# Two neighbouring state blocks' output products issued together, term by term, in the S5 branch of a two-layer mixer block

## The chip, the cores and the metric

One core of a Trainium2 chip runs the whole program. The metric is device time in microseconds (us) of one execution; below, a time without a unit is in us. Engines: PE is TensorE (matrix products; PEld is its weight load), DVE is VectorE, ACT is ScalarE, POOL is GpSimd, SP issues the transfers.

## What is computed

The program is two layers on 256 tokens of width 1024. Each layer normalises, projects, runs four mixers side by side (dilated attention, NSA attention, gated linear attention or GLA, and S5), normalises the four results, projects them out, and ends with a feed-forward part (a SwiGLU in layer 0, eight experts in layer 1). The change is in S5, whose reference is, cut to what matters:

```
bu = einsum(ug, bb)                      # 16 groups x 64 complex states, per token
x_re, x_im = scan over tokens of x[t] = abar * x[t-1] + bu[t]
y = einsum('bsgn,gcn->bsgc', x_re, c_re) - einsum('bsgn,gcn->bsgc', x_im, c_im)
y = y + d * u;  hg = gelu(y);  return hg * sigmoid(hg @ glu_w + glu_b)
```

## The kernel before

All inputs of S5 are f32. The 16 x 64 states of a layer are 1024 rows, worked in eight **state blocks** m = 0 to 7 of 128 rows each. Per block (`m_s5`, lines 853 to 878): two products bring in the inputs (tile `s5b`, line 858, one PSUM buffer); DVE turns them into the rotating frame (lines 864 to 867, tiles `s5t` and a second `s5t` that is only scratch), runs two scans (line 870), and multiplies back: `p1` (named `s5p`, line 872, on DVE) and `z` (named `s5t`, line 873, on POOL, by the table `S5OUT`). Tiles `s5p` and `s5t` have two buffers each.

Then come the **output products** (lines 874 to 877): four f32 products, the *terms* 0 to 3, with a stationary operand of 128 rows x 32 columns. Term 0 and term 3 read `s5p`; terms 1 and 2 read `s5t`. All four accumulate into the same 32 partitions of the PSUM tile `s5y`; the quarter of the array's columns that they use is q = m mod 4 (`tile_position=(0, 32 * q)`). In the trace each f32 product is two matmul records (two passes).

Everything before the experts is placed by a list scheduler: the text of a layer is generated in the order of the string `ORDER`, one letter per step of a generator (S is a step of `m_s5`), and the scheduler then sets each engine's queue from its own estimates, with the projections (`w_...` tiles, 128x256 or 128x512 products) as work to fill in. Each engine then works its queue strictly in that order. Where a step's instructions change, the places of many others change with it. The feed-forward parts have an order written by hand.

`chid` (line 1154) is the other place that uses 32-column products: its neighbours go round all four column quarters.

Of the kernel before, what the change touches and what calls it, by code (L numbers as in the profile page):

```python
# [258 lines left out]
class Build:  # L259
# [565 lines left out]
    def m_s5(self):  # L825
        tc, nc, l, sp = self.tc, self.nc, self.l, self.sp
        v, g = nc.vector, nc.gpsimd
        mag = self.s5c[:, 0, 8 * l:8 * l + 8]
        fr = self.s5c[:, 1, 8 * l:8 * l + 8, None].to_broadcast([P, 8, 32])
        fi = self.s5c[:, 2, 8 * l:8 * l + 8, None].to_broadcast([P, 8, 32])  # L830
        cc = sp.tile([P, 3, 8, 32], F32, name="s5cc")
        t = sp.tile([P, 2, 8, 32], F32, name="s5ct", tag="s5p1", bufs=2)
        cr = self.par_("cr").rearrange("p (m c) -> p m c", m=8)
        ci = self.par_("ci").rearrange("p (m c) -> p m c", m=8)
        g.tensor_mul(t[:, 0], cr, fr)
        g.tensor_mul(t[:, 1], ci, fi)
        g.tensor_sub(cc[:, 0], t[:, 0], t[:, 1])
        g.tensor_sub(cc[:, 1], t[:, 1], t[:, 0])
        g.tensor_mul(t[:, 0], cr, fi)
        g.tensor_mul(t[:, 1], ci, fr)  # L840
        g.tensor_add(t[:, 0], t[:, 0], t[:, 1])
        g.tensor_scalar(cc[:, 2], t[:, 0], -1.0, None, op0=ALU.mult)
        if l:
            tab = self.tab
        else:
            with tc.issue_after(self.last_lo):
                tab = self.s5_tables(l, sp)
        yield
        uT = self.r["uT"]
        br = self.par_("br").rearrange("p (u n) -> p u n", u=2)  # L850
        bi = self.par_("bi").rearrange("p (u n) -> p u n", u=2)
        yp = self.ps("s", [P, 2, S], "s5y")
        for m in range(8):
            u, q = m // 4, m % 4
            rr = slice(32 * q, 32 * q + 32)
            b = self.ps("b", [P, 2, S], "s5b")
            for i, w in enumerate((br, bi)):
                nc.tensor.matmul(b[:, i], w[rr, u, :], uT[rr, u, :], start=True, stop=True, skip_group_check=True,  # L858
                                 tile_position=(32 * q, 0))
            cb = tab[:, 0, m, None, :].to_broadcast([P, 2, S])  # L860
            sb = tab[:, 1, m, None, :].to_broadcast([P, 2, S])
            z = sp.tile([P, 2, S], F32, name="s5t1", bufs=2)
            t2 = sp.tile([P, 2, S], F32, name="s5t2", bufs=1)
            v.tensor_mul(z, b, cb)
            v.tensor_mul(t2, b, sb)
            v.tensor_add(z[:, 0], z[:, 0], t2[:, 1])
            v.tensor_sub(z[:, 1], z[:, 1], t2[:, 0])
            mb = mag[:, m:m + 1].to_broadcast([P, S])
            for i in range(2):
                v.tensor_tensor_scan(z[:, i], mb, z[:, i], 0.0, op0=ALU.mult, op1=ALU.add)  # L870
            p1 = sp.tile([P, 2, S], F32, name="s5p1", bufs=2)
            S5OUT[0](nc).tensor_mul(p1, z, cb)
            S5OUT[1](nc).tensor_mul(z, z, sb)
            o = yp[32 * q:32 * q + 32, u, :]
            for i, (w, x) in enumerate(((0, p1[:, 0]), (1, z[:, 1]), (2, z[:, 0]), (2, p1[:, 1]))):
                nc.tensor.matmul(o, cc[:, w, m, :], x, start=i == 0, stop=i == 3, skip_group_check=True,  # L876
                                 tile_position=(0, 32 * q))
            yield
        y = sp.tile([P, 2, S], F32, name="s5yy", tag="s5t1", bufs=2)
        d = self.par_("s5d")  # L880
        for u in range(2):
            v.scalar_tensor_tensor(y[:, u], uT[:, u], d[:, u:u + 1], yp[:, u], op0=ALU.mult, op1=ALU.add)
        hg = sp.tile([P, 2, S], F32, name="s5hg")
        self.gelu(hg, y, [P, 2, S])
        yield
        gw = self.par_("gw").rearrange("p (k n) -> p k n", k=2)
        gb = self.par_("gb")
        gp = self.ps("a", [P, 2, S], "s5gp")
        zt = sp.tile([P, 2, S], F32, name="s5zt", tag="s5p1", bufs=2)
        for m in range(2):  # L890
            for k in range(2):
                self.mm(gp[:, m], gw[:, k, P * m:P * m + P], hg[:, k], k == 0, k == 1)
            v.tensor_scalar(zt[:, m], gp[:, m], gb[:, m:m + 1], None, op0=ALU.add)
        self.sigm(zt, zt, [P, 2, S])
        v.tensor_mul(hg, hg, zt)
        self.dump(f"y5{l}", hg)
        yield
        self.mixnorm(hg, 3)
        yield
# [956 lines left out]
```

## Time and profile before

| | us |
|---|---|
| median of 3 runs | 1447.29 (1445.8 to 1450.13) |
| the profiled execution | 1446.44 |
| its span, first to last instruction | 1444.6 |
| PE busy | 1400.3 (97%) |
| DVE busy | 891.3 (62%) |
| ACT busy | 703.8 (49%) |
| POOL busy | 120.4 (8%) |

Of the span, 86% of the chain that ended last is PE; PE's share at line 876, the products of this change, is 2%. S5's blocks run from about 67 to 126 us (layer 0) and from 400 to 457 us (layer 1). From 600 us on there are only experts. A busy PE is counted with overlaps and modelled ends, so the cost of a product is better read from the distance between starts, which the chain of waits gives.

### The profile page before, as it was taken

To read this page: it belongs to the slowest core of one execution; us is meant where nothing else is said; L and a number is where in the kernel's file an instruction comes from. 1 tells how busy PE (TensorE), PEld (TensorE's weight loads), DVE (VectorE), ACT (ScalarE), POOL (GpSimd) and SP (SyncE) were. 2 spreads that over 40 slices of the span, in tenths; PEclk is the share of its full clock that TensorE was granted. 3 is DMA by queue.
4 is the path that set the end of the run, shared out by engine and by line. 5 is a ranking of instruction groups with operands and counts; after the bars stand their busy time and mean duration, and the time that the engine had idled before them with its cause. 6 is when DMAs were issued, how large, how long until landed. Compare 5 with 4: busy or idle time off the path is not lost.

```text
span 1444.6 us, 19381 instructions
## 1 busy us (share of the span) xinstructions
PE 1400.3 (97%) x7189; PEld 966.2 (67%) x7189; DVE 891.3 (62%) x1371; ACT 703.8 (49%) x1090; POOL 120.4 (8%) x100
## 2 busy tenths in 40 slices
PE   8899899999999998999999999999999999999997
PEld 6667789999867877765566555566555566655652
DVE  8876878555696676864556554556554556455541
ACT  5436466444524744754454544554544554445430
POOL 3235300000222223000000000000000000000000
PEclk9999999999999998999999999999999999999999
DMA  8513085554325217789999999999999999999992
GB/s 336 189 53 134 30 304 194 188 177 146 110 98 229 89 69 323 286 346 416 419 421 421 379 388 403 421 422 420 388 388 400 420 422 421 411 413 407 421 421 108
DMA packets 61731, 434.58 MB, mean 301 GB/s; under 512 B 7360, under 2 KB 7616, under 8 KB 9664
## 3 DMA queue, kind: packets, MB, share of 16 engines
q1 hardware_dynamic: 61200, 432.73, 74.5%
q8 instruction: 58, 0.95, 0.3%
q10 hardware_dynamic: 432, 0.56, 0.1%
q14 instruction: 41, 0.34, 0.1%
HBM read 432.22 MB, written 1.05 MB: 300 GB/s over the span
## 4 chain that ended last, share of the span: by engine, by line
PE 86%; DVE 7%; issue 2%; ACT 2%; POOL 1%; DMA 0%; ACTq 0%; DVEq 0%; POOLq 0%
PE mgu L271 20%; PE my L271 18%; PE mgus L271 14%; PE fgu L271 8%; PE fy L271 4%; DVE wlo L309 2%; PE s5y L876 2%; PE acc L271 2%; PE mht L1628 2%; PE w_gv L271 2%; PE mgat L271 1%; PE mco L271 1%; PE s5b L858 1%; PE w_dq L271 1%; PE w_dk L271 1%
## 5 line engine op out<-in xcount | busy, mean ns | idle before, releaser
L309 DVE TENSOR_TENSOR wlo<-raw,whi 128x1024 fp32r<-128x1024 f32 x447 | 542.1, 1235 | 212.3 <-ACT whi L306 208.4
L306 ACT ACTIVATE whi<-raw 128x1024 fp32r<-128x1024 f32 x456 | 471.4, 1057 | 217.1 <-PE my L271 43.2
L271 PE MATMUL mgu<-whi,X 128*128 128x512 f32 x892 | 290.2, 399 | 0.0
L271 PE MATMUL mgus<-raw,Xf 128*64 128x512 f32 x896 | 213.3, 597 | 0.0
L271 PEld LDWEIGHTS mgu<-whi,X 128*128 128x128 f32 x892 | 169.0, 189 | 40.7 <-issue 2.2
L271 PE MATMUL mgu<-wlo,X 128*128 128x512 f32 x446 | 179.7, 403 | 0.8 <-DVE wlo L309 0.8
L271 PEld LDWEIGHTS mgus<-raw,Xf 128*64 128x64 f32 x896 | 63.4, 137 | 118.5 <-issue 113.5
L271 PE MATMUL my<-raw,mhx 128*64 128x512 f32 x448 | 105.6, 599 | 0.6 <-DVE mhx L1644 0.6
L271 PEld LDWEIGHTS mgu<-wlo,X 128*128 128x128 f32 x446 | 84.6, 190 | 20.3 <-DVE wlo L309 1.4
L271 PE MATMUL fgu<-flo,whi 128*128 128x256 f32 x344 | 96.5, 281 | 0.2 <-DVE flo L537 0.2
L271 PE MATMUL fgu<-fhi,wlo 128*128 128x256 f32 x344 | 96.4, 280 | 0.0
L271 PE MATMUL fgu<-fhi,whi 128*128 128x256 f32 x344 | 96.3, 280 | 0.0
L1635 ACT ACTIVATE mhh<-mht 128x512 fp32r<-128x512 f32 x28 | 16.7, 597 | 159.2 <-PE mht L1628 159.2
L271 PE MATMUL my<-wlo,mhh 128*128 128x512 f32 x224 | 89.1, 398 | 0.3
L271 PE MATMUL my<-whi,mhl 128*128 128x512 f32 x224 | 88.9, 397 | 0.0
L271 PE MATMUL my<-whi,mhh 128*128 128x512 f32 x224 | 74.7, 407 | 0.0
L1636 DVE TENSOR_TENSOR mhl<-mht,mhh 128x512 fp32r<-128x512 f32 x28 | 19.3, 690 | 88.3 <-ACT mhh L1635 88.3
L1621 DVE TENSOR_TENSOR mh<-mh,mgu 128x512 f32<-128x512 f32 x28 | 19.3, 688 | 82.8 <-PE mgu L271 82.8
L271 PEld LDWEIGHTS my<-raw,mhx 128*64 128x64 f32 x448 | 30.3, 136 | 58.3 <-issue 50.5
L271 PEld LDWEIGHTS fgu<-flo,whi 128*128 128x128 f32 x344 | 64.7, 188 | 0.8 <-DVE flo L537 0.4
L271 PEld LDWEIGHTS fgu<-fhi,whi 128*128 128x128 f32 x344 | 64.6, 188 | 0.4
L271 PEld LDWEIGHTS fgu<-fhi,wlo 128*128 128x128 f32 x344 | 64.6, 188 | 0.0
(479 smaller groups left out, 2069.5 us busy)
## 6 DMA issues: line engine op xcount, KB each, us to landing
raw<-in_moe SPq DMA_DIRECT2D x335, 1024.0 KB, 10.6
raw<-in_ffn SPq DMA_DIRECT2D x32, 1024.0 KB, 4.8
raw<-in_win SPq DMA_DIRECT2D x19, 1024.0 KB, 4.9
raw<-in_cw SPq DMA_DIRECT2D x8, 1024.0 KB, 4.9
raw<-in_wout SPq DMA_DIRECT2D x8, 1024.0 KB, 6.8
ca<-in_ca SPq DMA_DIRECT2D x2, 1152.0 KB, 8.6
par<-in_par SPq DMA_DIRECT2D x2, 1081.5 KB, 12.1
gbig<-in_cg SPq DMA_DIRECT2D x2, 864.0 KB, 6.7
```

Of the source, the lines that this page charges most:

```text
L271: self.nc.tensor.matmul(out, lhsT, rhs, start=start, stop=stop, skip_group_check=True)
L306: self.last_hi = self.nc.scalar.activation(hi, r, AF.Copy).ins
L309: self.last_lo = eng.tensor_sub(lo, r, hi.bitcast(F32)).ins
L858: nc.tensor.matmul(b[:, i], w[rr, u, :], uT[rr, u, :], start=True, stop=True, skip_group_check=True, tile_position=(32 * q, 0))
L876: nc.tensor.matmul(o, cc[:, w, m, :], x, start=i == 0, stop=i == 3, skip_group_check=True, tile_position=(0, 32 * q))
L1621: later(lambda p=p: v.tensor_mul(h, h, p))
L1628: nc.tensor.transpose(t[:, j], h[:, j * P:j * P + P], idn)
L1635: later(lambda: nc.scalar.activation(hh, t, AF.Copy))
L1636: later(lambda: v.tensor_sub(hl, t, hh.bitcast(F32)))
```

## The change

The four output products of a block are no longer issued at the end of the block. Blocks are taken in pairs (0 and 1, 2 and 3, ...). The even block only keeps its operands; at the end of the odd block the eight products of both are issued term by term, even block first: term 0 of m, term 0 of m+1, term 1 of m, and so on. Neighbours in this order use different column quarters. Products, operands, sizes and buffers are the same.

```diff
+        pair = []
         for m in range(8):
...
-            o = yp[32 * q:32 * q + 32, u, :]
-            for i, (w, x) in enumerate(((0, p1[:, 0]), (1, z[:, 1]), (2, z[:, 0]), (2, p1[:, 1]))):
-                nc.tensor.matmul(o, cc[:, w, m, :], x, start=i == 0, stop=i == 3, skip_group_check=True,
-                                 tile_position=(0, 32 * q))
+            pair.append((m, ((0, p1[:, 0]), (1, z[:, 1]), (2, z[:, 0]), (2, p1[:, 1]))))
+            for i in range(4) if m % 2 else ():
+                for n, terms in pair:
+                    w, x = terms[i]
+                    q = n % 4
+                    nc.tensor.matmul(yp[32 * q:32 * q + 32, n // 4, :], cc[:, w, n, :], x, start=i == 0, stop=i == 3,
+                                     skip_group_check=True, tile_position=(0, 32 * q))
+            if m % 2:
+                pair = []
             yield
```

What the scheduler makes of it, at three places. First PE's queue at the first pair of layer 0; `s5p_939` and `s5t_931` are block 1 before:

```order
L876 MATMUL s5y<-s5p_939,s5cc 32x256
L271 MATMUL w_dk<-hhi,wlo 128x256
L271 MATMUL w_dk<-hhi,whi 128x256
L271 MATMUL w_dk<-hlo,whi 128x256
L271 MATMUL w_dk<-hhi,wlo 128x256
L876 MATMUL s5y<-s5t_931,s5cc 32x256 x2
L876 MATMUL s5y<-s5p_939,s5cc 32x256
```

In the changed program, on PE at the same pair, `s5p_921` and `s5t_913` are block 0, `s5p_935` and `s5t_927` block 1:

```order
L880 MATMUL s5y<-s5p_935,s5cc 32x256
L880 MATMUL s5y<-s5t_913,s5cc 32x256
L1125 MATMUL nt_967<-id,p_966 128x128
L880 MATMUL s5y<-s5t_927,s5cc 32x256
L880 MATMUL s5y<-s5t_913,s5cc 32x256
L880 MATMUL s5y<-s5t_927,s5cc 32x256
L880 MATMUL s5y<-s5p_921,s5cc 32x256
L880 MATMUL s5y<-s5p_935,s5cc 32x256
```

Block 0's term 0 still goes early and alone (some rows above); the other seven products of the pair now alternate. Each of the eight pairs reads like this: one product alone, then seven that alternate, in one piece (4 pairs) or cut by other work into two and five (4 pairs).

Second, PE's queue at the end of layer 0's S5. Before, block 7 (its inputs are this `s5b`) is only wanted some 40 rows further down, after the two w_gv projections, and block 6 (`s5p_1183`, `s5t_1175`) is next:

```order
L858 MATMUL s5b<-uT,par 128x256 x2
L271 MATMUL qms<-qsq,cst 128x512
L876 MATMUL s5y<-s5p_1183,s5cc 32x256
L1138 MATMUL nt_1193<-id,p_1192 128x128 x2
L271 MATMUL ns_1309<-kz,nqn 128x512
L876 MATMUL s5y<-s5t_1175,s5cc 32x256 x2
L876 MATMUL s5y<-s5p_1183,s5cc 32x256
```

In the changed program the same stretch of PE's queue, with block 7 as `s5p_1288` and `s5t_1280`:

```order
L859 MATMUL s5b<-uT,par 128x256 x2
L880 MATMUL s5y<-s5p_1183,s5cc 32x256
L271 MATMUL qms<-qsq,cst 128x512
L271 MATMUL ns_1309<-kz,nqn 128x512
L271 MATMUL ckc<-chT,par 128x16 x2
L271 MATMUL gz<-par,ag 128x128 x2
L880 MATMUL s5y<-s5p_1288,s5cc 32x256
L880 MATMUL s5y<-s5t_1175,s5cc 32x256
L880 MATMUL s5y<-s5t_1280,s5cc 32x256
```

Block 7's products have moved ahead of the w_gv projections, to a few rows behind the products that bring in its inputs.

Third, PE's queue where layer 0's GLA begins, behind the last projection (w_gr). `gd` and `gL` are GLA's first products, `s5gp` is S5's gate, `ds` and `dt` are dilated attention. Before:

```order
L271 MATMUL gd<-cst,gqk 128x4 x2
L271 MATMUL gL<-gbig,glz 128x2x128 x2
L271 MATMUL s5gp<-s5hg,par 128x256 x2
L271 MATMUL ds_1453<-kz,qn 128x256 x2
L271 MATMUL gL<-gbig,glz 128x2x128 x2
```

After, on PE at the same place:

```order
L271 MATMUL s5gp<-s5hg,par 128x256 x2
L271 MATMUL ds_1453<-kz,qn 128x256 x2
L271 MATMUL s5gp<-s5hg,par 128x256 x2
L271 MATMUL gd<-cst,gqk 128x4 x2
L271 MATMUL ds_1476<-kz,qn 128x512
L1048 MATMUL dt_1465<-id,p_1456 128x128
L271 MATMUL ds_1494<-kz,qn 128x512
L1048 MATMUL dt_1465<-id,p_1456 128x128
L271 MATMUL gL<-gbig,glz 128x2x128
```

GLA's first `gL` has moved behind S5's gate and behind all three score products of dilated attention.

## Rows read from the trace of the kernel before

**Rows 1.** The page's slices: busy tenths of PE in 40 equal slices of the span

```profile
PE   8899899999999998999999999999999999999997
```

**Rows 2.** Stretches: us, then busy us (count) per engine, granted clock, DMA share, GB/s

```profile
67.00:126.00 59.00, 59.00 (x301) 36.77 (x293) 42.27 (x98) 23.82 (x62) 23.44 (x17) 1.00 0.29 105
126.00:189.00 63.00, 55.82 (x307) 45.33 (x308) 48.61 (x97) 35.33 (x83) 25.11 (x17) 1.00 0.24 86
189.00:380.00 191.00, 188.97 (x1323) 174.44 (x1321) 116.98 (x184) 98.96 (x156) 2.32 (x3) 1.00 0.53 189
...
400.00:457.00 57.00, 56.89 (x369) 38.75 (x368) 46.44 (x74) 15.13 (x27) 14.81 (x13) 1.00 0.38 141
457.00:503.00 46.00, 46.00 (x285) 38.65 (x284) 29.79 (x72) 35.53 (x79) 9.60 (x8) 1.00 0.38 144
...
600.00:1444.60 844.60, 831.44 (x3669) 497.22 (x3667) 460.95 (x476) 398.05 (x499) 0.00 (x0) 1.00 0.96 395
```

The busy columns are PE, PEld, DVE, ACT and POOL.

**Rows 3.** The chain of waits in order of time: start, us, engine, tile, records

```profile
76.29 0.55 PE s5y L876 x2
...
77.51 1.41 PE s5y L876 x6
...
96.29 1.84 PE s5y L876 x8
...
406.17 0.67 PE w_nq L271 x4
...
408.25 2.09 PE w_nq L271 x16
```

**Rows 4.** Tile s5y's records: count, ns min/median/max, first and last start

```profile
L876 PE MATMUL s5y<-s5p,s5cc x64: 379/379/404, 67.8 to 452.1; 128*32 128x256 f32 x64
```

There is a second row like it, for the terms that read s5t, with 64 records too.

**Rows 5.** The chain again, where products go round all four column quarters

```profile
66.09 1.86 PE chid L271 x32
```

**Rows 6.** Tile s5t's records, as in Rows 4: POOL's part of a block

```profile
L873 POOL TENSOR_TENSOR s5t<-s5t,s5tab x16: 1269/1281/3338, 64.5 to 449.2; 128x512 f32<-128x512 f32 x16
```

**Rows 7.** Timeline of DVE, layer 0's kz and layer 1's block 7: start, us, instruction

```profile
111.19 0.75 DVE L1028 SCALAR_TENSOR_TENSOR kz<-w_dk,par,qr 128x512 f32<-128x512 f32 x1 [1.82 <-ACT qr L331]
...
445.08 0.69 DVE L864 TENSOR_TENSOR s5t<-s5b,s5tab 128x512 f32<-128x512 f32 x1 [1.56 <-PE s5b L858]
...
448.38 0.69 DVE L872 TENSOR_TENSOR s5p<-s5t,s5tab 128x512 f32<-128x512 f32 x1
```

**Rows 8.** The chain in layer 0, products that now stand ahead of block 7

```profile
107.97 1.06 PE qms L271 x2
...
109.95 0.86 PE ns L271 x2
...
115.88 0.44 PE gz L271 x4
```

**Rows 9.** Timeline of ACT and DVE: steps of S5's gelu, layers 0 and 1

```profile
132.30 0.73 ACT L812 ACTIVATE s5hg<-s5hg,one 128x512 f32<-128x512 f32 x1
...
452.57 0.87 DVE L882 SCALAR_TENSOR_TENSOR s5yy<-uT,par,s5y 128x256 f32<-128x256 f32 x2 [0.97 <-PE s5y L876]
...
457.50 0.43 DVE L810 TENSOR_SCALAR s5hg<-s5hg 128x512 f32<-128x512 f32 x1
```

**Rows 10.** The chain in layer 1 at S5's gate

```profile
463.47 0.86 PE s5gp L271 x4
```

**Rows 11.** Timeline of layer 0 where GLA begins, several engines

```profile
133.11 0.53 PEld L271 LDWEIGHTS gd<-cst,gqk 128*128 128x128 f32 x4
...
135.15 0.60 ACT L942 ACTIVATE gE<-gL 128x512 f32<-128x512 f32 x1
...
136.80 4.40 POOL L952 TENSOR_TENSOR gQ<-gq,gE 128x512 f32<-128x512 f32 x2
```

**Rows 12.** Weight loads at the round of quarters: the tile's records, and the timeline

```profile
L271 PEld LDWEIGHTS chid<-raw,blk x128: 106/110/155, 43.3 to 447.5; 128*32 128x32 f32 x128
...
66.02 1.45 PEld L271 LDWEIGHTS chid<-raw,blk 128*32 128x32 f32 x32
```

## The prediction

> **What bounds the kernel now.** I read the slices first: PE is at eight or nine tenths nearly everywhere [rows 1]. Then the stretches, with their granted clock: it is 1.00, the full 2.4 GHz, in all of those shown. In S5's two, PE is busy all the time (59.00 of 59.00 us, 56.89 of 57.00), and so it is in what follows them, the feed-forward of layer 0 (188.97 of 191) and the rest of layer 1's projections (46.00 of 46) [rows 2]. So time that S5 gives back on PE can reach the end, as long as PE does not start to wait. DVE comes second: 42.27 of 59 us in layer 0 and 46.44 of 57 in layer 1 [rows 2]. The stretch from 126 to 189 us is different: PE has 7 us idle there, and GLA's recursion goes through ACT, POOL and DVE. The experts from 600 us on are PE's too (831.44 of 844.60), and their first loads follow the end of the mixers, so they should move as a whole.
>
> **What a product costs.** The output products are two rows of 64 records, 128 in all [rows 4]: 64 products, two records each. In the chain one product takes 0.55, three take 1.41, four take 1.84 [rows 3]: 0.43 for each further product, so a run of them costs 0.43 a product and 0.12 to begin. Coming back to full-width work costs too: 4 products of w_nq behind a run take 0.67 and 16 take 2.09 [rows 3], that is 0.118 a product and 0.20 once. A run thus costs 0.32 besides its products. All of it lies on PE's path.
>
> **What alternating gives.** The trace before has no two neighbours in two quarters, but it has four: in chid, 32 records, which are 16 products of the same shape, take 1.86 [rows 5]. Less 0.12 that is 0.109 a product, a quarter of 0.43. So four quarters run at once, and I take it that two quarters run two at once: 0.43 for two products. The bounds are 0.43 a product (nothing overlaps) and 0.215; chid is the nearest row, so I take 0.215 where two neighbours can pair.
>
> **The sum on PE.** Before, 64 x 0.43 = 27.5, in 29 runs counted in PE's order (14 and 15), x 0.32 = 9.3: 36.8. After, each of the eight pairs is one product alone (0.43) and seven that alternate, which make four steps of 0.43 (the seventh has no partner; cut into two and five it is one and three steps): 2.15 a pair, 17.2 in all; the runs are 20 (10 and 10), 6.4. That is 23.6, and 13.2 less. In two places the two input products of a block are cut apart by other work, which adds two runs, 0.6. **Gross: 12.6**, of it about 6.1 in layer 0 and 6.5 in layer 1.
>
> **What is given back.** The pair brings new waits. Term 1 of the odd block reads a tile that POOL writes in 1.28, starting when DVE ends `s5p` [rows 6]. PE starts the seven at that moment, has one step (0.55) to do and then waits, with all its queue behind it: 1.28 + 0.07 (a hand-over) - 0.55 = 0.8 where nothing stands between, less where a cut puts other work there. By the order that is 0.5 (an nt product between), 0.1 and 0.8 for layer 0's first three pairs, and 0.8, 0.2, 0.8, 0.2 in layer 1, where before the first block already stood about 0.4 for POOL: 1.4 and 1.6 net. Before, this wait was covered by three or four projection products, and in several pairs the cover is gone.
>
> The last pair of layer 0 is worse. Block 7's inputs come in only just ahead of its products. From them DVE takes 4.0 to the end of `s5p` (445.08 to 448.38 + 0.69 for the same block of layer 1, undisturbed) [rows 7]; a `kz` operation of 0.75 [rows 7] stands in its queue between, and I add 0.05 for the hand-over: 4.8. PE has in between one product alone with its run (0.75), qms 0.86 to 1.06, ns 0.86, ckc about 0.35 and gz 0.44 [rows 8]: 3.3. So PE waits 1.5, then 0.8 more for POOL: 2.3. Bounds: 1.0, if `kz` costs nothing, and 4.0 if POOL is as slow as its slowest record, 3.34.
>
> S5's gate in layer 1: from the last `s5y`, whose end released `s5yy` at 452.57 [rows 9], to `s5gp` at 463.47 [rows 10] PE had 11 us of other work. By its new order it has 45 products of w_dk at 0.118, qms and gz: 5.3 + 0.9 + 0.4, some 6.7. The gelu between takes 5.4 to the end of line 810 (457.93) [rows 9], then three ACT steps of up to 0.73 [rows 9] and a multiplication like those of a block, 2.7 at most: 8. That leaves 1.3; since weight splits queued among these steps may move, I put 1.0, between 0 and 2.
>
> The two buffers of `s5t`: the next pair's first operation on DVE (line 865 now) overwrites a tile that the pair's term 2 must have read, so DVE stands in its queue until PE is there, and behind it stand weight splits that PE's projections need. By the order one or two such splits and other work stand ahead of it in layer 1, which covers the 2.3 that POOL and two steps of PE take. I put nothing; without that cover it is 1 to 2 a pair (a rival below). Transfers: SP's order is the same, nothing moves there.
>
> Given back: 1.4 + 2.3 + 1.6 + 1.0 = 6.3, between 3 and 9. **Net 6.3**: 2.4 in layer 0, 3.9 in layer 1.
>
> **The GLA stretch of layer 0.** There the order changed beyond S5. Before, GLA's first `gE` came 2.0 after the last projection product (133.11 to 135.15), and POOL's `gQ` was then busy to 141.2 [rows 11]. Now the first `gL` stands behind S5's gate (4 records, 0.86, twice), ds three times (0.86 each), gd and dt, and `gE` behind the attention's exponentials on ACT: about 9 after the last projection product instead of 2. Against it, the attention, S5's gate and the gelu are then out of the way of the later steps. It is a recursion in which every step waits for ACT, POOL, PE and DVE in turn, with 7 us of PE idle. I take nothing for it, with -2 to +7 as bounds.
>
> **Sum.** Against its own time, the profiled execution's 1446.44 becomes 1446.44 - 6.3 = 1440.1. It lies 0.85 below the median of the runs, so the median should be **1441.0**, 0.44% faster. A change of 0.3% (4.3) is about what a measurement of this kernel can tell from none.
>
> **Rivals.** *GLA's late start eats layer 0's gain.* For: `gE` is 7 later relative to the projections and the recursion has few parallel branches. Against: the branches that it competed with are done earlier. If 4 to 7 of the 7 reach the end of the stretch, layer 0 loses 1.6 to 4.6 and layer 1 still gains 3.9: 1445 to 1448, within 0.3%. 20%.
>
> *DVE becomes the bound through the two buffers: slower.* In layer 1 DVE's 46.44 make 11.6 a pair, against 14.25 a pair of the stretch [rows 2]. If the standing adds over 2.65 a pair, DVE sets the pace. POOL's 1.28 and PE's two steps add 2.3; with POOL slowed by DVE to 3.34 [rows 6] it is 4.4, so 1.7 a pair, 7 in layer 1, instead of a gain; with layer 0's 2.4 left the time is about 1452. What speaks against it is the work queued ahead of the blocked operation, and that the slow record of POOL is one of 16. 10%.
>
> *No overlap of two quarters.* The products would stay at 0.43 each; only the nine runs fewer remain (2.3 net of the cut input products), which the waits take back: 1447. The Trainium skill, TensorE: Matmul & The Clock Gate, Part 3, has a rule that speaks for it: a weight load overlaps with matmuls in flight only when the row group differs. All eight products of a pair use the same rows. By that rule the loads would stand open and take the overlap back. What the rows show, as a mechanism here: the 32 loads of chid, also all of the same rows, last 0.11 each, 3.5 in all, but are done within 1.45 [rows 12], less than the 1.86 of the products [rows 5]. So by the trace the loads do not stand open, and I leave it 4%.
>
> *More than forecast.* If the waits are covered, or the GLA stretch gains by what was cleared ahead of it, up to 12.6 and 2 more: 1433 to 1435. 8%.
>
> **How the numbers follow.** The forecast, a gain of 4.3 to 12, has 58%; with the last rival faster by over 0.3% is 66%. Within 0.3%: 20 + 4 = 24%. Slower: 10%. The range goes from 1435 (a gain of 12, most waits covered) to 1448 (GLA's late start in full).
>
> **What would show it.** In the changed trace, seven alternating products take about 1.84 in the chain where four took 1.84; their records start in twos, 0.215 apart. Line 880 takes about 24 of PE's path with its switches, not 37. PE shows waits for POOL at line 874 of up to 0.8 in most pairs, and one of about 1.5 for `s5p` near the end of layer 0's S5. Layer 0's feed-forward starts 2 to 3 earlier and the router of layer 1 6 earlier; the experts take as long as now. I am wrong if records in two quarters start one after the other, if DVE idles at line 865 for over 1 a pair, or if the GLA stretch of layer 0 grows by more than 3.

## The result

The change made the kernel slower: 1455.41 us (1453.34 to 1457.65) against 1447.18 (1445.8 to 1450.13), a ratio of 1.0056 [1.0045, 1.0066]. I had forecast 1441.0, within 1435 to 1448. The profiled execution has a span of 1455.6 us against 1444.6. One traced execution can lie some us from its kernel's median (e3's, below, took 1447.21, its median is 1443.01), so below the medians say how much, and the traces where.

The page's slices of the changed kernel (40 slices of 36.4 us; PE's busy tenths, and the granted clock in tenths of full speed) answer [rows 1]. They differ in the fourth to the sixth slice, from 109 to 218 us, where PE is at 8, 7 and 8 instead of 9, 8 and 9; in the fourth the clock is at 8:

```profile
PE   8898789999999998999999999999999999999997
...
PEclk9998999999999998999999999999999999999999
```

The stretches say more. The columns are those of [rows 2]: busy time of PE, PEld, DVE, ACT and POOL, granted clock, DMA share, GB/s:

```profile
67.00:126.00 59.00, 54.95 (x310) 34.38 (x309) 46.31 (x102) 22.24 (x59) 20.23 (x15) 0.97 0.23 87
126.00:189.00 63.00, 51.97 (x266) 43.17 (x265) 41.84 (x85) 30.87 (x73) 26.92 (x17) 0.89 0.17 60
133.00:142.50 9.50, 9.47 (x58) 9.45 (x59) 2.21 (x4) 4.42 (x9) 1.69 (x1) 0.70 0.20 83
142.50:160.00 17.50, 15.77 (x70) 12.26 (x68) 8.70 (x27) 11.28 (x29) 9.24 (x7) 0.80 0.17 60
400.00:457.00 57.00, 55.41 (x401) 42.18 (x400) 46.73 (x73) 18.89 (x31) 12.28 (x13) 0.99 0.34 119
457.00:503.00 46.00, 45.80 (x289) 36.72 (x288) 31.51 (x76) 31.49 (x72) 9.21 (x8) 1.00 0.44 173
```

PE now has 4.05 us idle in S5's stretch of layer 0, where it had none, and from 126 to 189 the clock is 0.89 on average instead of 1.00 [rows 2]. Between 133 and 160 us PE is nearly always busy (9.47 of 9.50, 15.77 of 17.50) at 0.70 and 0.80: by these means some 13 of the 27 us were at 1.2 GHz, half speed.

The chain of waits (start, us, what) shows the place where it turns:

```profile
119.91 1.27 PE s5y L880 x4
121.19 1.81 PE w_gv L271 x6
...
125.71 2.89 DVE s5hg L821
...
128.62 2.46 DVE s5hg L810
...
131.11 0.64 ACT s5hg L811
...
131.77 0.72 ACT s5hg L812
132.49 0.49 ACT gv L750
...
133.03 1.86 PE w_gr L271 x7
```

S5's products are done at 121.2, some four us earlier than before, and gv's at 128.6. PE has a few small products left, up to 129.6, and then stands still for the evacuation of gv by ACT (line 750), since w_gr is to be written into a buffer that gv holds (timeline of PE):

```profile
133.03 0.58 PE L271 MATMUL w_gr<-whi,hhi 128*128 128x256 f32 x1 [3.40 <-ACT gv L750]
```

ACT could have evacuated at 128.6, but in its queue two steps of S5's gelu (lines 811 and 812) now stand ahead, and they wait for DVE. The timeline of ACT in the kernel before, and then in the changed one (start, us, instruction, and in brackets what ended ACT's idle time):

```profile
122.66 1.29 ACT L750 ACTIVATE gv<-w_gv 128x512 f32<-128x512 f32 x2 [0.58 <-PE w_gv L271]
...
131.66 0.61 ACT L811 ACTIVATE s5hg<-s5hg 128x512 f32<-128x512 f32 x1
```

```profile
131.11 0.63 ACT L811 ACTIVATE s5hg<-s5hg 128x512 f32<-128x512 f32 x1 [3.77 <-DVE s5hg L810]
131.77 0.72 ACT L812 ACTIVATE s5hg<-s5hg,one 128x512 f32<-128x512 f32 x1
132.40 1.06 ACT L750 ACTIVATE gv<-w_gv 128x512 f32<-128x512 f32 x2
```

Before, gv was evacuated right behind its products, and the gelu came 9 us later. Now the gelu is first, ACT idles 3.77 for it, and PE waits for ACT. It could pass gv because S5 now ends before gv's products do, and that the change itself has done.

The gelu was late for a reason of its own, too. Its two steps on DVE (lines 821 and 810) stood beside two weight splits of POOL. The timelines of POOL and of DVE in the changed kernel, and then DVE's before:

```profile
125.62 2.41 POOL L309 TENSOR_TENSOR wlo<-raw,whi 128x1024 fp32r<-128x1024 f32 x1 [7.26 <-ACT whi L306]
128.00 2.79 POOL L309 TENSOR_TENSOR wlo<-raw,whi 128x1024 fp32r<-128x1024 f32 x1
```

```profile
125.71 2.88 DVE L821 TENSOR_TENSOR s5hg<-s5hg,s5yy 128x512 f32<-128x512 f32 x1
128.62 2.45 DVE L810 TENSOR_SCALAR s5hg<-s5hg 128x512 f32<-128x512 f32 x1
```

```profile
127.74 0.69 DVE L821 TENSOR_TENSOR s5hg<-s5hg,s5yy 128x512 f32<-128x512 f32 x1
...
130.72 0.41 DVE L810 TENSOR_SCALAR s5hg<-s5hg 128x512 f32<-128x512 f32 x1
```

With 0.69 and 0.41 in place of 2.88 and 2.45 the gelu's two steps on ACT would have been through at about 128.6, just as gv's products end, and PE, busy to 129.6, would not have waited. That is an estimate from these rows; no run takes the splits out of the changed kernel.

All the kernels below are compared by four stretches, each from one profiled execution, read from the first and last records of w_qag, w_gr, x (line 639) and w_uT: **S** from the last w_qag to the first w_gr of layer 0 (S5's stretch, with the wait), **W** the products of w_gr, **G** from there to the first addition to x (GLA, attention, output), and **L1**, in layer 1, from the first w_uT to the last w_gr (S5's stretch there). The last column is the granted clock in S and in G.

| kernel | S | W | G | S+W+G | L1 | clock in S, G |
|---|---|---|---|---|---|---|
| before | 59.9 | 7.4 | 55.1 | 122.4 | 86.8 | 1.00, 1.00 |
| changed | 64.7 | 9.4 | 60.9 | 135.0 | 82.6 | 0.96, 0.94 |
| e1, pairs in layer 1 | 59.8 | 7.4 | 55.1 | 122.4 | 83.4 | 1.00, 1.00 |
| e2, pairs in layer 0 | 63.2 | 9.4 | 62.6 | 135.2 | 86.9 | 0.99, 0.92 |
| e3, gelu behind gv | 61.0 | 6.8 | 57.5 | 125.3 | 83.3 | 0.97, 0.97 |
| e4, not alternated | 66.7 | 9.4 | 62.5 | 138.6 | 86.8 | 0.99, 0.92 |
| e5, GLA late | 59.6 | 6.8 | 62.3 | 128.7 | 83.3 | 1.00, 0.95 |
| e6, before, gv behind gelu | 68.8 | 7.4 | 48.2 | 124.4 | 87.0 | 1.00, 1.00 |
| e7, GLA early | 61.2 | 6.8 | 60.9 | 128.9 | 82.6 | 0.97, 0.92 |
| e8, filled wait | 67.4 | 5.9 | 60.2 | 133.5 | 82.6 | 1.00, 0.97 |
| e9, GLA's first step early | 60.1 | 6.8 | 62.1 | 128.9 | 83.3 | 1.00, 0.89 |
| e10, GLA among w_gr | 60.1 | 12.5 | 57.6 | 130.2 | 82.5 | 1.00, 0.91 |
| e11, e3 with other terms | 59.5 | 6.8 | 56.5 | 122.8 | 82.3 | 1.00, 1.00 |
| e12, e10 with other terms | 61.0 | 12.5 | 57.6 | 131.1 | 81.8 | 0.97, 0.91 |
| e13, e11 with splits on DVE | 59.5 | 6.8 | 56.4 | 122.7 | 82.3 | 1.00, 1.00 |
| e14, e1 with other terms | 59.9 | 7.4 | 55.1 | 122.4 | 82.6 | 1.00, 1.00 |

So the changed kernel gains 4.2 in layer 1 and loses 12.6 in layer 0: 3.4 in the wait, 1.4 in the rest of S, 1.9 in W and 5.8 in G. The 1.4 is the clock's, in this trace: from 117 to 121 us it was 0.65. In e2, with the same order of PE and ACT in layer 0 and the same waits, it was 1.00 there, and S without the wait is 59.8. The stretch in the changed kernel, then in e2:

```profile
117.00:121.00 4.00, 3.19 (x14) 1.03 (x14) 1.36 (x6) 1.09 (x4) 1.27 (x1) 0.65 0.36 126
```

```profile
117.00:121.00 4.00, 3.99 (x21) 2.72 (x22) 1.67 (x5) 1.53 (x5) 0.00 (x0) 1.00 0.65 221
```

G is 56.5 or less in every trace with its clock at 1.00 there, and 57.5 or more in every other. So a part of what G loses below may be the clock's and not the order's; no run tells the two apart.

### The profile page after: what moved, and what is told of

It is laid out like the page before. It is cut to its first block, busy times and chain, and to the rows that moved or that the text cites. A ratio compares the mean times of both kernels' runs of the same rounds, so it can differ in the third digit from the quotient of the medians.

```text
span 1455.6 us, 19381 instructions
## 1 busy us (share of the span) xinstructions
PE 1398.8 (96%) x7189; PEld 968.5 (67%) x7189; DVE 895.5 (62%) x1371; ACT 703.8 (48%) x1090; POOL 118.7 (8%) x100
## 4 chain that ended last, share of the span: by engine, by line
PE 84%; DVE 9%; ACT 3%; issue 2%; DMA 1%; POOL 1%; SPq 0%; ACTq 0%; POOLq 0%; DVEq 0%
PE mgu L271 20%; PE my L271 18%; PE mgus L271 14%; PE fgu L271 8%; PE fy L271 4%; DVE wlo L309 2%; PE acc L271 2%; PE mht L1634 2%; PE mgat L271 1%; PE mco L271 1%; PE s5y L880 1%; PE w_gv L271 1%; ACT whi L306 1%; PE w_gr L271 1%; PE w_dq L271 1%
## 5 line engine op out<-in xcount | busy, mean ns | idle before, releaser
L1627 DVE TENSOR_TENSOR mh<-mh,mgu 128x512 f32<-128x512 f32 x28 | 19.2, 687 | 82.5 <-PE mgu L271 82.5
L271 PEld LDWEIGHTS fgu<-flo,whi 128*128 128x128 f32 x344 | 64.7, 188 | 0.8 <-DVE flo L537 0.4
```

The source lines that it names most:

```text
L271: self.nc.tensor.matmul(out, lhsT, rhs, start=start, stop=stop, skip_group_check=True)
L1627: later(lambda p=p: v.tensor_mul(h, h, p))
```

## The experiments

The theories: **A**, the order on ACT behind S5 in layer 0 makes the loss, by PE's wait at w_gr and the lower clock behind it; **B**, the pairs' own waits eat the gain, in either layer; **C**, GLA's late start in layer 0 is the loss.

**e1, pairs in layer 1 alone, and e2, in layer 0 alone.**

```diff
-            for i in range(4) if m % 2 else ():
+            for i in range(4) if m % 2 or not l else ():
...
-            if m % 2:
+            if m % 2 or not l:
                 pair = []
```

(e2 has `or l` in both lines.)

> Pairs in layer 1 alone; layer 0 issues as in the kernel before. Theory A (the loss is made in layer 0, behind S5: the gelu's ACT steps stand ahead of gv's two evacuations, PE waits 3.4 for them and then runs at a lower clock): layer 1 keeps its 3.7, so 1447.2 - 3.7 = 1443.5, 0.997 of before. Theory B (the pairs' own waits for POOL and DVE eat the gain wherever a pair stands, and layer 1's 3.7 only came from its starting 14.8 later): 1447, no difference. Theory C (GLA's late start in layer 0 is the loss): as A, 1443.5.

> Pairs in layer 0 alone; layer 1 issues as before. Theories A and C: all of the loss and none of layer 1's gain: 1455.4 + 3.7 = 1459, 1.008 of before; the first gE comes about 10 after the last w_gr. Theory B: half of a loss that both layers share, 1451.

Measured: e1 1443.8 us, 0.9974 [0.9963, 0.9984]; e2 1461.15, 1.0100 [1.0081, 1.0120]. In e1 stretches S, W and G are those of the kernel before; in e2 PE waits 3.4 at w_gr again, and L1 is that of before. So layer 1's gain is real and does not come from a late start there, the whole loss is layer 0's, and theory B falls as its cause. In layer 0 it holds for the gain, though: S without the wait is 59.8 in e2, where before has 59.9.

**e3, the gelu's ACT steps behind gv's evacuations (layer 0).**

```diff
+            self.gvi = nc.scalar.activation(gv[:, T], pv[T], AF.Copy).ins
-            nc.scalar.activation(gv[:, T], pv[T], AF.Copy)
...
-        self.gelu(hg, y, [P, 2, S])
+        with ExitStack() as cx:
+            if not l:
+                cx.enter_context(tc.issue_after(self.gvi))
+            self.gelu(hg, y, [P, 2, S])
```

> The changed kernel with one bound more: in layer 0 the gelu's ACT steps are issued behind gv's two evacuations. Theory A: PE's 3.4 ahead of w_gr is gone and with it the fall of the clock behind it, so the last w_gr is back within 2 of the kernel before's 133.1 (it was at 142.4): 9 to 11 come back, 1444 to 1446. Theory B: the pairs are untouched, so the time stays at 1455. Theory C: only what GLA's order gains; PE's wait ahead of w_gr goes but the clock does not come back, 1449 to 1452, and the stretch from the last w_gr to the mixers' end still takes 61.

Measured: 1443.01 us, 0.9968 [0.9959, 0.9977]: 12.4 less than the changed kernel. ACT's timeline and the stretches behind it:

```profile
127.00 1.31 ACT L750 ACTIVATE gv<-w_gv 128x512 f32<-128x512 f32 x2 [0.98 <-PE w_gv L271]
```

```profile
126.00:133.00 7.00, 7.00 (x56) 6.63 (x55) 5.53 (x11) 4.90 (x11) 4.11 (x3) 1.00 0.53 188
133.00:142.50 9.50, 7.99 (x44) 6.17 (x43) 6.89 (x17) 7.41 (x15) 7.66 (x5) 1.00 0.49 181
```

gv is evacuated as soon as its products are there, PE is busy all the time from 126 to 133, and the clock is 1.00 there and up to 142.5. The last w_gr ends at 135.3 instead of 142.4. But the edit also moved GLA: its first gE starts 5.5 behind the last w_gr, against 9.9 in the changed kernel and about 2 in the one before, and other steps of the attention and GLA with it. So e3 alone does not tell theory A from C; e5 does.

**e4, the pairs without alternating.**

```diff
-            for i in range(4) if m % 2 else ():
-                for n, terms in pair:
+            for n, terms in pair if m % 2 else ():
+                for i in range(4):
```

> The products of a pair stay behind the odd block's scan in the program, but block by block, so that neighbours share a column quarter; PE's queue has block 7 ahead of gv's second half as in the changed kernel, and the gelu's ACT steps ahead of gv's evacuations. If alternating is worth what I put (0.43 for two): eight pairs by 3 steps of 0.43 more, 10.3, less the waits of the pairs that go, 3 to 6, so 1459 to 1463 by theory A, which keeps the loss behind S5. Theory B (the waits of alternating pairs are the loss): those are gone and the time is back at 1447 or less. Theory C: as A.

Measured: 1464.81 us, 1.0112 [1.0090, 1.0134], a little above what I expected. It has the changed kernel's order on ACT, the 3.4 at w_gr and a clock of 0.64 and 0.81 behind it, and nothing of the gain: L1 is 86.8, as before. Against it the changed kernel is 9.4 faster, which is what alternating is worth: the table shows 7.8 of it, 3.6 in layer 0 and 4.2 in layer 1. So the overlap works, and what costs is the grouping of the blocks.

**e5, e3 with GLA late, as in the changed kernel.** The first gE is issued behind the attention's second `pt` on ACT.

```diff
+            with ExitStack() as cx:
+                if not self.l and lp == 0:
+                    cx.enter_context(tc.issue_after(self.dpt))
+                nc.scalar.activation(E, L.rearrange("p a b c -> p a (b c)"), AF.Exp, scale=1.0 / 16)
-            nc.scalar.activation(E, L.rearrange("p a b c -> p a (b c)"), AF.Exp, scale=1.0 / 16)
...
+            pti = nc.scalar.activation(pt, t, AF.Copy).ins
+            self.dpt = pti if tl == 0 else self.dpt
-            nc.scalar.activation(pt, t, AF.Copy)
```

> The kernel of e3, in which PE's wait ahead of w_gr is gone, but with GLA's first exponential held back behind the attention's second evacuation on ACT, where the changed kernel has it (gE 9.9 after the last w_gr instead of e3's 5.5). If GLA's late start has a price of its own (theory C as a second part of the loss), the stretch from the last w_gr to the mixers' end grows from e3's 57.5 to about 62 and the time from 1443 to 1447 or 1448. If the wait and the clock were all of it (theory A alone), the stretch stays within 1 of e3's and the time at 1443.

Measured: 1448.01 us, 1.0002 [0.9992, 1.0012], 5.0 above e3. G grew from 57.5 to 62.3, with no wait at w_gr and the clock at 1.00 from 126 to 142.5. The first gE came 11.9 behind the last w_gr, two us later than in the changed kernel, and steps of the attention changed places on ACT with it. So theory C is a second part of the loss: of the 12.4 between e3 and the changed kernel some 5, at that delay, belong to the order with GLA late, and the other 7 to the wait and the clock.

**e6, the kernel before with gv behind the gelu, without any pair.** gv's evacuation is written behind the gelu, which moves p_gr there too.

```diff
+        if not self.l:
+            yield
...
+            if not self.l:
+                cx.enter_context(self.tc.issue_after(self.gelu_ln))
...
-"...NvvSDNCrSMSDDDGG..."
+"...NvvSDNCSvrMSDDDGG..."
```

> The kernel before, without any pair, with gv's evacuations of layer 0 issued behind the gelu's first two ACT steps; GLA's first gL move ahead of w_gr on PE by it, so GLA starts no later than before. Theory A, in its strong form (the order on ACT alone makes the loss, whatever S5's products cost): PE waits 5 or more ahead of w_gr, the clock falls behind it, the last w_gr ends about 9 later than 133.4; GLA's early start gives up to 4 back: 1451 to 1456. If the pairs are needed for the loss: 1447, no wait at w_gr and a clock of 1.00 from 133 to 160.

Measured: 1449.8 us, 1.0014 [1.0005, 1.0024]. The first half came as expected: of PE's waits, and of its chain,

```profile
PE w_gr L271 <- ACT gv L755: 4.0, 1, 4.0
```

```profile
134.04 7.42 PE w_gr L271 x48
```

The order on ACT makes this wait without any pair, and the last w_gr ends 8.1 later. But the time rose by 2.2 only: with gv late, gL and gE had gone ahead of w_gr, and G shrank by 7 to 48.2, more than the 4 that I had allowed. So the order on ACT is enough for the wait; most of the loss did not come with it where GLA was early.

**e7, e3 with GLA ahead of S5's gate and the attention.**

```diff
-"...NvvSDNCrSMSDDDGGCDD..."
+"...NvvSDNCrSMGGSDDDCDD..."
```

> The kernel of e3 with GLA's two first steps written ahead of S5's gate and the attention, so that gL and gE come directly behind the last w_gr, as gE did in the kernel before (2 behind it). If the late start is what keeps layer 0 from its gain: the stretch to the mixers' end goes from 57.5 to 55 and the time to 1440 or 1441. If the attention, which is now later, becomes the last branch instead: 58 or more, 1443 to 1446.

Measured: 1447.21 us, 1.0000 [0.9991, 1.0010]: the gain of e3 is gone, and more than I had put for that case. gE comes 2.8 behind the last w_gr, but G is 60.9: the attention is late now (its first ds 11.7 behind the last w_gr, 2.2 in e3), PE is busy for 6.64 of 9.50 from 133 on, and the clock is 0.64 there. That the attention is what makes G long is read from this, not shown by a run.

**e8, products put into the wait of the changed kernel.**

```diff
+            if h == 3 and not self.l:
+                fp = self.ps("s", [P, 2, S], "fill")
+                for i in range(8):
+                    with self.tc.issue_after(self.fill):
+                        self.fill = nc.tensor.matmul(fp, idn, r["uT"], start=True, stop=True, skip_group_check=True).ins
...
```

> The changed kernel with eight products more on PE (128x512, 0.86 each, their result unused) where it waited for gv's evacuation; the queue behind them is as in the changed kernel, but for cms, cvc and four no products that come ahead of w_gr. If the idle time is what brings the clock down: it stays 1.00 from 133 to 160, the 48 products of w_gr take 7.0 instead of 9.35, though they start 2 later, and the time is 3 to 4 less than the changed kernel's: 1451 to 1453. If the clock falls for another reason: 0.70 and 0.80 as in the changed kernel, w_gr takes 9.4, 1456 to 1458.

Measured: 1454.3 us, 1.0044 [1.0027, 1.0061], 1.1 less than the changed kernel. Its chain and its stretches:

```profile
124.31 6.87 PE fill L1152 x16
...
132.68 5.72 PE w_gr L271 x48
```

```profile
133.00:142.50 9.50, 9.26 (x64) 8.20 (x64) 4.18 (x16) 5.12 (x10) 2.90 (x2) 1.00 0.23 74
142.50:160.00 17.50, 13.82 (x76) 10.16 (x76) 11.49 (x32) 10.92 (x34) 11.96 (x9) 1.00 0.05 20
```

With PE busy the clock stays at 1.00 up to 160 and w_gr takes 5.7 (without its four no products, which come ahead). Over the whole span it is 0.986 or 0.987 in all four runs, against 0.980 to 0.984 in the six of the changed kernel. So the idle time did bring the clock down. But the return is small: S is 2.7 longer, since the eight products take 6.9 where PE had waited 3.4, and G is nearly as long as in the changed kernel (60.2 against 60.9). I had expected 3 to 4.

**e9, e3 with GLA's first step ahead of w_gr, and e10, with the first two.**

```diff
-"...NvvSDNCrSMSDDDGGCDD..."
+"...NvvSDNCGrSMSDDDGCDD..."
...
+"...NvvSDNCGGrSMSDDDCDD..."
```

> The kernel of e3 with GLA's first step written ahead of w_gr in layer 0, so that behind the last w_gr PE has gL, s5gp, ds in the order of the kernel before, and ACT the first gE ahead of S5's gate. With the wait at w_gr and GLA's lateness both gone, only the pairs themselves are left in layer 0: by my prediction 2.4 gained there and 3.9 in layer 1, 1447.5 - 6.3 = 1441; if layer 0's S5 gains nothing (as its stretch in e3's trace, 61.0 against 59.9, would have it), 1443.5 to 1444.

> The kernel of e3 with GLA's first two steps written ahead of w_gr, so that gL and the first gE come among the products of w_gr, 5 or more earlier than in the kernel before. If the mixers' end hangs on GLA's start (e3 to e5: 4.5 later, 5.0 lost; the e6 kernel: 7 earlier, 7 of the stretch given back): 4 to 6 below 1443, 1437 to 1439. If the attention or S5's gate, now later on ACT, becomes the last branch as it did in e7: 1443 to 1446.

Measured: e9 1450.21 us, 1.0011 [1.0000, 1.0022]; e10 1451.22, 1.0023 [1.0013, 1.0033]. Both missed on the far side. For e9 the clock has a part in it: its ten runs go from 1445.29 us, at a granted clock of 0.988 over the span, to 1453.15 at 0.979. In e9 gL follows the last w_gr at 134.7, but on ACT the gelu is ahead of the first gE and waits for DVE again; ACT's timeline, and one of PE's waits:

```profile
135.96 0.63 ACT L811 ACTIVATE s5hg<-s5hg 128x512 f32<-128x512 f32 x1 [2.88 <-DVE s5hg L810]
...
139.34 0.59 ACT L951 ACTIVATE gE<-gL 128x512 f32<-128x512 f32 x1
```

```profile
PE s5gp L271 <- DVE s5hg L823: 3.2, 1, 3.2
```

In e10, PE's waits are inside w_gr, whose products stand behind GLA's in PE's queue (W is 12.5):

```profile
PE gL L271 <- ACT gE L951: 2.6, 1, 2.6
PE gs L271 <- POOL gQ L961: 2.6, 2, 2.3
```

So "earlier is better" does not hold for GLA: e5 is later than e3 and loses, e7, e9 and e10 are earlier and lose too.

**e11, e3 with the two terms that need only s5p first, and e12, e10 with the same.**

```diff
-            pair.append((m, ((0, p1[:, 0]), (1, z[:, 1]), (2, z[:, 0]), (2, p1[:, 1]))))
+            pair.append((m, ((0, p1[:, 0]), (2, p1[:, 1]), (1, z[:, 1]), (2, z[:, 0]))))
```

> The kernel of e3 with the four terms of a block in another order, the two that need only s5p first and the two that POOL writes last: PE has two steps more to do while POOL multiplies, so its five waits for POOL (3.6 in both layers in e3) should fall to 1 or less: 1443 - 2.6 = 1440.4. If something else is as late at these places: 1443.

> e10 and e11 together. If the two gains are of different stretches and add up: e10's time less 2.6, some 1435 to 1436; if not, the better of the two.

Measured: e11 1441.52 us, 0.9958 [0.9944, 0.9972]; e12 1450.27, 1.0013 [1.0003, 1.0023]. In e11 the waits for POOL's s5t are 1.8 in all (1.1 in layer 0, 0.7 in layer 1) instead of 3.6, and L1 is 1.0 shorter; PE's waits for DVE's s5p in layer 0 rose from 2.0 to 3.5. e12 is 1 below e10. The terms help by 1.0 in L1; that they help the whole time rests on this, since the intervals of e3 and e11 overlap, and so do those of e10 and e12.

**e13, e11 with w_gr's two weight splits on DVE, and e14, e1 with e11's terms in layer 1.**

```diff
-LO = ("vvvvgvvvvvvgvvvvgvggvvvvgvvg", "v" * 28)
+LO = ("vvvvgvvvvvvgvvvvgvvvvvvvgvvg", "v" * 28)
...
-            for i in range(4) if m % 2 or not l else ():
+            for i in ((0, 3, 1, 2) if l else range(4)) if m % 2 or not l else ():
...
-start=i == 0, stop=i == 3,
+start=i == 0, stop=i == (2 if l else 3),
```

> The kernel of e11 with the two weight splits of w_gr in layer 0 on DVE instead of POOL; the orders of PE and ACT are the same row for row. If POOL's splits slow the gelu's steps on DVE (0.41 became 2.45 and 0.69 became 2.88 beside them in the changed kernel): none of the gelu's steps on DVE takes over 1.3, the gelu in layer 0 takes 5.4 to 6.5 instead of 7.9, and PE's wait of 1.2 for it at s5gp goes: 1440 to 1441 (e11: 1441.5). If DVE's queue was the cause and not POOL, the two splits of 1.22 make the gelu later still: 1443 to 1444.

> Pairs in layer 1 alone, as in e1, with e11's order of terms there; layer 0 as in the kernel before. What e11 has over this is what pairs are worth in layer 0 with the evacuations kept ahead of the gelu. If layer 0 gains the 2.4 that I forecast: this has 0.9969 to 0.9972 of before (e1's 0.9974 less 0.7 us) against e11's 0.9958. If layer 0 gains nothing and the terms gained more in layer 1 than the trace shows: this has 0.996.

Measured: e13 1442.0 us, 0.9968 [0.9956, 0.9979], no better than e11; e14 1440.88, 0.9958 [0.9944, 0.9973], as much as e11 and the best of all, with the plain order of layer 0. The gelu's step of line 820 in e11 and then in e13:

```profile
128.21 1.22 DVE L820 TENSOR_SCALAR s5hg<-s5hg 128x512 f32<-128x512 f32 x1
```

```profile
126.36 0.42 DVE L820 TENSOR_SCALAR s5hg<-s5hg 128x512 f32<-128x512 f32 x1
```

That step is faster without POOL's splits, but from it to the end of the gelu it is 7.1 instead of 7.2, and PE's wait at s5gp 1.0 instead of 1.2. So those two splits are not what sets the gelu's length in e11. A third split of POOL's stays beside the gelu's last step (line 823), which takes 1.70 in both, against 0.69 in the changed kernel. Whether the splits set the gelu's length in the changed kernel was not tried. And since e14 has what e11 has, pairs in layer 0 are worth nothing that these runs can tell from zero, even without the wait and with better terms; S+W+G (122.8 in e11, 122.4 in e14) says the same.

## Why the prediction was wrong

**What a product costs, and the overlap: right.** The timeline of PE in the changed kernel, layer 0's last pair (start, us, records; in brackets the idle time ahead):

```profile
116.98 0.40 PE L880 MATMUL s5y<-s5p,s5cc 128*32 128x256 f32 x1 [1.12 <-DVE s5p L873]
116.99 0.40 PE L880 MATMUL s5y<-s5t,s5cc 128*32 128x256 f32 x1
117.22 0.38 PE L880 MATMUL s5y<-s5p,s5cc 128*32 128x256 f32 x1
117.23 0.38 PE L880 MATMUL s5y<-s5t,s5cc 128*32 128x256 f32 x1
118.42 0.64 PE L880 MATMUL s5y<-s5t,s5cc 128*32 128x256 f32 x2 [0.81 <-POOL s5t L874]
```

Records start in twos, the twos 0.24 apart. The chain, layer 1:

```profile
434.00 0.56 PE s5y L880 x4
...
435.23 1.41 PE s5y L880 x10
```

Two products take 0.56 where one took 0.55, and five take the 1.41 that three took [rows 3]: 0.12 and three steps of 0.43, as I had it for a pair cut into two and five. In layer 1 all runs of S5's output products, added up from the first start of each to the next other record, are 11.5 us in e1 with their waits, in 11 runs (I had counted 10), and were 15.6 in 15. The rival without overlap is out. The rule of the Trainium skill, TensorE: Matmul & The Clock Gate, Part 3, by which weight loads overlap with products in flight only where the row group differs, would have taken the overlap away, since all these products use the same rows. The trace does not agree: five products took 1.41, as three did, so the measurement decides.

**The pairs' waits: right.** PE's waits, in S5's stretch of layer 0 and then of layer 1 (us in total, times, longest):

```profile
PE s5y L880 <- POOL s5t L874: 2.1, 3, 0.8
PE s5y L880 <- DVE s5p L873: 2.0, 3, 1.1
```

```profile
PE s5y L880 <- POOL s5t L874: 1.5, 2, 0.8
```

For layer 0 I had 2.2 for POOL (1.4 and the last pair's 0.8) and 1.5 for DVE, for layer 1 1.6. The gate of layer 1, for which I had put 1.0, cost 0.2.

**Layer 1: right.** Forecast 3.9; measured 4.2 in the changed kernel, 3.4 in e1's trace, and 3.8 by e1's median. DVE did not become the bound through the two buffers.

**Layer 0 ahead of w_gr: the step that failed, its path behind S5.** I followed the new order on PE (the last pair, the waits for DVE and POOL) and stopped where S5's products ended. Behind them I took the projections to run on as before, and of the gelu I wrote that it is "out of the way of the later steps". I did not read ACT's new order, in which the gelu's steps had passed gv's evacuations; the price was the 3.4 and, by the clock, the 1.9 in W. Nor did I ask what DVE would do: I had the gelu's steps there at their undisturbed length, 0.43 for line 810 [rows 9], and 2.88 and 2.45 beside POOL's splits is what made the gelu late enough to hold gv, by the estimate above. e3 puts gv first, and the wait and the fall of the clock at w_gr are gone; e6 makes the wait without any pair. The size of what was missed, with what the clock adds, is some 7 us (the changed kernel against e5).

**The GLA stretch of layer 0: mechanism seen, value wrong.** I had the delay right (about 9 behind the last projection product; it was 9.9) and its bounds too (-2 to +7), and took zero, since I held the cleared gelu and gate against it. It cost 5.8 in the trace, more than the 3 that I had named as a sign of being wrong; e5 shows 5.0 for it without the wait, at a start 2 later still. What of it is GLA's waiting and what the clock's (0.94 in G) stays open. My first rival priced this at 4 to 7, with 20%, but left the rest of layer 0's gain standing, so that even it ended at 1448. The case that came was that rival and the wait together, and no case of mine had both.

**The gain that stays in layer 0: mis-sized.** I had 2.4 for S5's own stretch. With the clock at 1.00 and without the wait, S+W is 66.4 in e5 and 66.3 in e11, where it was 67.3: 1.0. And G gives that back, even in e11 (56.5 against 55.1). Of the other 1.4 of S5's stretch 0.4 is in waits that the trace names (2.1 and 2.0 against 2.2 and 1.5). Another 0.4 is in S5's runs in layer 0: they take 11.8 in e5's trace, with 1.6 of waits inside them, where my prices and these waits give 11.4 (15.4 before, as my prices have it). Where the rest went I did not find.

## What to carry over

Where a change lets one branch end earlier, read the new order on every engine up to the next place where the bounding engine needs a buffer back: a step of the early branch that now stands ahead of an evacuation in an in-order queue can cost more than the branch gained, above all if that step waits for yet another engine. Issue neighbouring narrow products into different column quarters where the rest of the order stays as it was (here layer 1: 0.9974, and 0.9958 with the terms that wait for another engine put last; the two intervals overlap), and leave it where the order around it is finely set. Price the rivals together as well as one by one.

## What the hardware did that I had not expected

- Behind PE's idle time of 3.4 us at w_gr there were two spells at the lower level of the clock, with the full clock between them, though PE was busy in them (the changed kernel; PE's busy time first, the clock before the last two columns):

```profile
133.00:138.70 5.70, 5.67 (x26) 5.67 (x27) 1.59 (x4) 3.27 (x7) 0.00 (x0) 0.50 0.33 138
138.70:152.30 13.60, 12.06 (x72) 9.17 (x70) 7.46 (x25) 10.72 (x27) 7.47 (x5) 1.00 0.22 77
152.30:159.10 6.80, 6.61 (x26) 6.16 (x27) 1.14 (x2) 1.22 (x3) 3.46 (x2) 0.50 0.00 0
```

  In the first the products of w_gr start 0.21 apart, behind it 0.12; that cost W 2.6 us (9.4 against 6.8 in e3). 7 us of idle time in small pieces, none over 1.9, from 126 to 189 left the clock at 1.00 in the kernel before [rows 2]. Eight products put into the gap kept it at 1.00 up to 160 (e8), so the gap made the first spell. The second is not shown to come from it: e5, without that gap, also has a lower clock in G (0.95). What the low clock costs in G stays open: G is only 0.7 shorter in e8, while e9's runs differ by 7.9 us along with the clock.
- A step of the gelu on DVE that ran beside a weight split of POOL ended just behind that split. In the changed kernel lines 821 and 810 ended 0.6 and 0.3 behind the two splits, after 2.88 and 2.45; in e9 line 810 took 2.60 and ended 0.3 behind a split of 2.48. Apart from them the two take 0.69 and 0.41. For line 820 e13 shows it (1.22 in e11, 0.42 with that split on DVE); for the changed kernel no run does.
